# Softmax weights of token tiles 1 to 3 folded into the transposing product by diagonal matrices

## The chip, the cores and the metric

The kernel runs on one core of one Trainium2 chip. The metric is the time of one execution in device microseconds (us), the median of a few runs. The engines are PE (TensorE, matrix products; PEld is its loading of the stationary operand), DVE (VectorE), ACT (ScalarE), POOL (GpSimd, here the issuer of the gathers) and SP (issues the plain DMAs). Each works through its own queue of instructions in order and waits there for semaphores.

## What is computed

One decoder layer over 512 tokens of width 1024: a projection; sparse attention (8 heads in 2 groups of 4, three branches: compressed, selected and window keys, each with a gate) beside a state-space branch; an output projection; and a PEER mixer, in which each token fetches 128 of 16384 experts. What the change touches is the attention's weighting of the values:

```python
def masked_softmax(s, mask):
    s = jnp.where(mask, s, NEG_INF)
    m = jnp.max(s, axis=-1, keepdims=True)
    e = jnp.where(mask, jnp.exp(s - m), 0.0)
    return e / jnp.maximum(jnp.sum(e, axis=-1, keepdims=True), 1e-30)
...
    p_s = masked_softmax(s_s, m_s)
    o_s = jnp.einsum('bghqnk,bgqnkd->bghqd', p_s, v_sel)
...
    return gb[..., 0:1] * o_c + gb[..., 1:2] * o_s + gb[..., 2:3] * o_w
```

With 8 blocks of 64 keys in 512 tokens, all blocks are selected, so the selected branch and the window branch are both causal attention over all earlier keys.

## The kernel before

The tokens stand in four tiles T of 128. Tiles 0 and 1 get their experts by gathers: for each of the 128 experts per token an indirect DMA fetches 128 rows of 8 KB, DVE forms the dot product with the token (`ISA junk`, the row `CUSTOM_DVE_ANT_0` of the profile), ACT the gelu in five small instructions on one column, and DVE adds the weighted value row (`SCALAR_TENSOR_TENSOR X<-X,act`). One such round is called a step here; `peer` (line 1070) makes them, over a ring of five buffers. Tiles 2 and 3 get theirs in `dense` (line 1215), which runs through all experts in 128 rounds and has the steps that are left of tile 1 woven in.

The steps of tile 0 run beside all that tiles 1 to 3 need before their experts: `rest` (line 1461) makes projections, `attention(1)`, the state-space output `glu_out`, the output projection `mix_out`, then, in `later` (line 1512), `attention(2)`, `attention(3)` and the output projection of both, interleaved with `route` of tile 1 (queries, and top-k on DVE), and last `route` of tiles 2 and 3. A credit count (line 1544) says after which piece of `rest` a step is written; it counts pieces, not time. The order on each engine is then set by a scheduler (line 1647), which moves instructions by its own estimate of their durations. All compute instructions are issued by one helper, so the profile gives them all line 134 and they are told apart by tile and shape.

In `attention(T)` (line 692) there are four blocks: two groups g of heads times two branches br. `scores` (line 721) makes for each of four heads the scores in a PSUM bank (PE), their maximum `nm` (DVE), the exponentials `Pt` with their sums `sm` (ACT); then DVE turns `sm` into gate over sum in three small instructions. Then each head's `Pt`, 128 x N with N = 128 (T + 1), is multiplied by its column of `sm`: on ACT for tile 3 and on DVE otherwise (`PSC`, line 688). `pv` (line 745) follows one block later. For each 128 keys it transposes the four heads on PE into one bank, copies the bank to SBUF (`PT`), and multiplies with the values into the bank `O`. `M.S()` gives out a 2 KB slot of a pool that every stage shares; `identb`, `ident` are identity matrices.

Of the kernel before, what the change touches and what calls it, by code (L numbers as in the profile page):

```python
# [18 lines left out]
AF = mybir.ActivationFunctionType  # L19
ALU = mybir.AluOpType  # L20
# [143 lines left out]
def hymba_kernel(ctx: ExitStack, tc: tile.TileContext, a, out, dbg=None):  # L164
    nc = tc.nc
    pins = set()
    V, S, G, PE = (Ordered(tc, e, n, pins) for e, n in ((nc.vector, "V"), (nc.scalar, "S"), (nc.gpsimd, "G"), (nc.tensor, "PE")))
# [10 lines left out]
    def tap(name, src):  # L178
        if name in dbg:
            SP.dma_start(dbg[name], src)  # L180
# [10 lines left out]
    M = Memory([base[:, 8192 * i:8192 * i + 8192] for i in (1, 2, 3, 0)]  # L191
               + [ep.tile([128, 8192], F32, name="X4"), ep.tile([128, 4096], F32, name="X5")])
# [4 lines left out]
    def bank():  # L197
        return pool[0].popleft()

    def bfree(*bs):  # L200
        pool[0].extend(bs)
# [11 lines left out]
    def b3(b, n):  # L213
        return b.rearrange("p (a b) -> p a b", b=n)

    def const(name, shape, dt=F32, eng=None):
        t = cst.tile(shape, dt, name="c_" + name)
        (eng or SP).dma_start(t, a[name])
        return t
# [60 lines left out]
    ident = const("ident", [128, 128])  # L280
# [404 lines left out]
    kcF, vcF = ct("kcF", [128, 2, 31]), ct("vcF", [31, 2, 64])  # L685


    PSC = lambda T, h: T > 2
    PCP = lambda T, kb: T < 3 and kb % 2
    AT, ST, XN, EI, GA = {}, {}, {}, {}, {}  # L690

    def attention(T):
        N = 128 * (T + 1)
        n31 = 7 if T == 0 else 31
        kcT, vcn = (kc0, vc0) if T == 0 else (kcF, vcF)
        ob = bank()
        O = b3(ob, 128)

        pcs = [bank(), bank()]
        for h in range(8):  # L700
            rows = slice(64 * (h % 2), 64 * (h % 2) + 64)
            PE.matmul(b3(pcs[h % 2], 128)[:, h // 2, 0:n31], qT[T][rows, h // 2], kcT[rows, h // 4], start=True, stop=True)
        scl = M.S()
        sc = scl.v([128, 8, n31])
        mx = tiny.tile([128, 8], F32, name="mx")
        sh = [128, 8, n31]
        for par in range(2):
            V.tensor_tensor(sc[:, par::2], b3(pcs[par], 128)[:, :, 0:n31], cmpb[:, T, 0:1, 0:n31].to_broadcast([128, 4, n31]), op=ALU.add)
        bfree(*pcs)
        V.reduce_max(mx, sc, axis=AX.X)  # L710
        V.tensor_tensor(sc, sc, mx[:, :, None].to_broadcast(sh), op=ALU.subtract)
        S.activation(sc, sc, AF.Exp)
        V.tensor_tensor(sc, sc, cmpb[:, T, 1:2, 0:n31].to_broadcast(sh), op=ALU.mult)
        V.reduce_sum(mx, sc, axis=AX.X)
        V.tensor_scalar(mx, mx, 1e-30, None, op0=ALU.max)
        V.reciprocal(mx, mx)
        V.tensor_tensor(mx, mx, gts[:, T, :, 0], op=ALU.mult)
        V.tensor_tensor(sc, sc, mx[:, :, None].to_broadcast(sh), op=ALU.mult)
        yield

        def scores(g, br):
            pl = M.S() if T == 0 else M.L((0, 1))
            Pt = pl.v([128, 4, N])
            nm = tiny.tile([128, 4], F32, name="nm")
            sm = tiny.tile([128, 4], F32, name="sm")
            for h in range(4):
                par, i = h % 2, h // 2
                ps = bank()
                rows = slice(64 * par, 64 * par + 64)
                PE.matmul(ps[:, 0:N], qT[T][rows, 2 * g + i], KT[rows, 2 * br + g, 0:N], start=True, stop=False)  # L730
                PE.matmul(ps[:, N - 128:N], identb, maskb, start=False, stop=True)
                V.reduce_max(nm[:, h:h + 1], ps[:, 0:N], axis=AX.X, negate=True)
                S.activation(Pt[:, h], ps[:, 0:N], AF.Exp, bias=nm[:, h:h + 1], accum_out=sm[:, h:h + 1])
                bfree(ps)
            V.tensor_scalar(sm, sm, 1e-30, None, op0=ALU.max)
            V.reciprocal(sm, sm)
            V.tensor_tensor(sm, sm, gts[:, T, 4 * g:4 * g + 4, 1 + br], op=ALU.mult)
            for h in range(4):
                if PSC(T, h):
                    S.activation(Pt[:, h], Pt[:, h], AF.Copy, scale=sm[:, h:h + 1])  # L740
                else:
                    V.tensor_scalar(Pt[:, h], Pt[:, h], sm[:, h:h + 1], None, op0=ALU.mult)
            return pl, Pt

        def pv(g, br, pl, Pt):
            for kb in range(T + 1):
                b = bank()
                pt = b3(b, 128)
                for h in range(4):
                    PE.transpose(pt[:, 2 * (h % 2) + h // 2], Pt[:, h, kb * 128:kb * 128 + 128], ident)  # L750
                ps = M.S()
                PT = ps.v([128, 4, 128])
                if PCP(T, kb):
                    V.tensor_copy(PT, pt)
                else:
                    S.activation(PT, pt, AF.Copy)
                bfree(b)
                for par in range(2):
                    PE.matmul(O[64 * par:64 * par + 64, 2 * g:2 * g + 2], VC[:, kb, 128 * br + 64 * g:128 * br + 64 * g + 64],
                              PT[:, 2 * par:2 * par + 2], start=(br == 0 and kb == 0), stop=False, skip_group_check=True)  # L760
                M.free(ps)
                yield
            M.free(pl)

        prev = None
        for g in range(2):
            for br in range(2):
                cur = (g, br) + scores(g, br)
                yield
                if prev:  # L770
                    yield from pv(*prev)
                    if prev[1] == 1:
                        yield from cmp_pv(prev[0], sc, vcn, O, n31)
                prev = cur
        yield from pv(*prev)
        yield from cmp_pv(1, sc, vcn, O, n31)
        M.free(scl)
        al = M.S()
        aT = al.v([128, 4, 128])
        S.activation(aT, O, AF.Copy)  # L780
        bfree(ob)
        AT[T] = (al, aT)
        tap(f"aT{T}", aT)
        yield

    def cmp_pv(g, sc, vcn, O, n31):
        b = bank()
        pt = b3(b, 128)
        for h in range(4):
            PE.transpose(pt[0:n31, 2 * (h % 2) + h // 2], sc[:, 4 * g + h], ident)  # L790
        ps = M.S()
        PC = ps.v([n31, 4, 128])
        S.activation(PC, pt[0:n31], AF.Copy)
        bfree(b)
        for par in range(2):
            PE.matmul(O[64 * par:64 * par + 64, 2 * g:2 * g + 2], vcn[:, g], PC[:, 2 * par:2 * par + 2],
                      start=False, stop=True, skip_group_check=True)
        M.free(ps)
        yield
# [851 lines left out]
```

## Time and profile before

| what | value |
| --- | --- |
| median of 3 runs | 1618.69 us (1617.03 to 1622.68) |
| the profiled execution, its own time | 1620.03 us |
| its span, first to last instruction | 1618.2 us |
| DVE busy, share of the span | 91% |
| PE busy, share of the span | 84% |
| ACT busy, share of the span | 52% |
| mean DMA rate | 290 GB/s |

The span falls into a prologue with tile 0 (to about 300 us), the stretch of steps beside `rest` (to about 870 us) and `dense` (the rest). A busy share over the whole span says little about a change that acts between 370 and 600 us; there the stretches have to be read one by one. "PEclk" is the TensorE clock that was granted, as a share of 2.4 GHz: 0.5 is its low level of 1.2 GHz. Records of a PE product end where a model puts it, so back-to-back counts are more to be trusted than single lengths.

### The profile page before, as it was taken

To read this page: it belongs to the slowest core of one execution; us is meant where nothing else is said; L and a number is where in the kernel's file an instruction comes from. 1 tells how busy PE (TensorE), PEld (TensorE's weight loads), DVE (VectorE), ACT (ScalarE), POOL (GpSimd) and SP (SyncE) were. 2 spreads that over 40 slices of the span, in tenths; PEclk is the share of its full clock that TensorE was granted. 3 is DMA by queue.
4 is the path that set the end of the run, shared out by engine and by line. 5 is a ranking of instruction groups with operands and counts; after the bars stand their busy time and mean duration, and the time that the engine had idled before them with its cause. 6 is when DMAs were issued, how large, how long until landed. Compare 5 with 4: busy or idle time off the path is not lost.

```text
span 1618.2 us, 24071 instructions
## 1 busy us (share of the span) xinstructions
PE 1367.1 (84%) x8256; PEld 1081.8 (67%) x8256; DVE 1475.7 (91%) x3392; ACT 837.0 (52%) x2046; POOL 521.8 (32%) x383
## 2 busy tenths in 40 slices
PE   5687794588946689696579999999999999999996
PEld 2366572454433455682358888888888999999995
DVE  8986279969899999699999999999999999999998
ACT  2335523545455675225565555555555556555553
POOL 6422013745354233003002333333333433333331
PEclk9897898787877789899859999999999999999998
DMA  6331478888998989309707999999999999999994
GB/s 263 104 105 65 169 278 295 330 321 300 375 352 297 345 356 370 152 6 343 248 4 262 338 345 332 342 337 340 333 346 357 392 375 377 374 375 379 375 376 171
DMA packets 88967, 469.45 MB, mean 290 GB/s; under 512 B 10253, under 2 KB 10893, under 8 KB 50701
## 3 DMA queue, kind: packets, MB, share of 16 engines
q0 software_dynamic: 37152, 268.98, 42.7%
q1 hardware_dynamic: 51692, 198.94, 34.3%
q8 instruction: 64, 1.05, 0.2%
q14 instruction: 59, 0.48, 0.1%
HBM read 464.74 MB, written 3.15 MB: 289 GB/s over the span
## 4 chain that ended last, share of the span: by engine, by line
DVE 46%; PE 29%; issue 12%; DMA 6%; ACT 3%; POOL 3%; SPq 0%; DVEq 0%; POOLq 0%; ACTq 0%
PE bank L134 29%; DVE X L134 27%; DVE lo L134 8%; DVE junk L134 7%; DMA X<-in_uv,eidx 5%; POOL X L134 2%; ACT X L134 2%; DVE act L134 1%; DVE nm L134 1%; DVE more L134 1%; DMA X<-in_x 0%; ACT gt L134 0%; DMA raw<-in_uvt 0%; DVE zT L134 0%; DVE hid L134 0%
## 5 line engine op out<-in xcount | busy, mean ns | idle before, releaser
L134 POOL DMA_INDIRECT X<-in_uv,eidx x256 | 431.6, 1686 | 967.0 <-DVE X L134 854.1
L134 ACT ACTIVATE X<-bank 128x256 f32<-128x256 f32 (+5 forms) x423 | 213.4, 518 | 184.0 <-PE bank L134 134.3
L134 PE MATMUL bank<-hi,act 128*128 128x512 f32 x1024 | 299.7, 394 | 0.0
L134 PE MATMUL bank<-XH,hi 128*128 128x256 f32 x1024 | 288.9, 282 | 4.1 <-ACT hi L134 4.1
L134 PE MATMUL bank<-XH,lo 128*128 128x256 f32 x1024 | 287.8, 281 | 0.0
L134 PE MATMUL bank<-XL,hi 128*128 128x256 f32 x1024 | 287.5, 281 | 0.0
L134 PE MATMUL bank<-X 128*128 128x64 f16 (+10 forms) x1768 | 235.9, 283 | 59.6 <-DVE X L134 39.7
L134 DVE CUSTOM_DVE_ANT_0 junk<-X 128x1024 bf16<-128x1024 f32 x206 | 250.8, 1217 | 14.0 <-DMA X<-in_uv,eidx 11.0
L134 ACT ACTIVATE gt<-hid 128x1 f32<-128x1 f32 x384 | 63.8, 198 | 363.1 <-DVE hid L134 362.9
L134 DVE TENSOR_TENSOR X<-X 128x256 f32<-128x256 f32 (+13 forms) x611 | 230.6, 410 | 22.5 <-ACT X L134 19.7
L134 DVE SCALAR_TENSOR_TENSOR X<-X,act 128x1024 f32<-128x1024 f32 x194 | 247.6, 1276 | 3.6 <-ACT act L134 3.6
L134 DVE TENSOR_TENSOR lo<-raw,hi 128x1024 fp32r<-128x1024 f32 x172 | 209.4, 1217 | 2.8 <-ACT hi L134 2.8
L134 PEld LDWEIGHTS bank<-hi,act 128*128 128x128 f32 x1024 | 183.3, 188 | 32.6
L134 PEld LDWEIGHTS bank<-XH,hi 128*128 128x128 f32 x1024 | 193.9, 189 | 9.1 <-ACT hi L134 4.2
L134 PEld LDWEIGHTS bank<-XL,hi 128*128 128x128 f32 x1024 | 193.3, 189 | 4.9
L134 PE MATMUL bank<-X,X 128*128 128x128 f32 (+7 forms) x888 | 177.1, 373 | 20.9 <-ACT X L134 12.9
L134 PEld LDWEIGHTS bank<-XH,lo 128*128 128x128 f32 x1024 | 194.2, 190 | 0.0
L134 ACT ACTIVATE hi<-raw 128x1024 fp32r<-128x1024 f32 x172 | 179.0, 1053 | 27.4 <-PE bank L134 21.8
L134 PEld LDWEIGHTS bank<-X,X 128*128 128x128 f32 (+4 forms) x888 | 119.8, 194 | 66.2 <-issue 29.7
L134 PE MATMUL bank<-lo,act 128*128 128x512 f32 x512 | 159.5, 393 | 0.4 <-DVE lo L134 0.4
L134 PEld LDWEIGHTS bank<-X 128*128 128x128 f32 (+3 forms) x744 | 117.5, 197 | 54.9 <-issue 28.5
L134 PE MATMUL bank<-c_ident,X 128*128 128x128 f32 (+2 forms) x300 | 55.6, 337 | 85.4 <-DVE X L134 49.4
(202 smaller groups left out, 1775.2 us busy)
## 6 DMA issues: line engine op xcount, KB each, us to landing
raw<-in_uvt SPq DMA_DIRECT2D x172, 512.0 KB, 7.0
X<-in_uvt SPq DMA_DIRECT2D x84, 512.0 KB, 6.7
X<-in_wq SPq DMA_DIRECT2D x24, 1024.0 KB, 8.9
X<-in_wo SPq DMA_DIRECT2D x8, 1024.0 KB, 7.7
X<-in_x SPq DMA_DIRECT2D x8, 512.0 KB, 3.7
X<-in_wB SPq DMA_DIRECT2D x4, 1024.0 KB, 12.8
X<-in_wA SPq DMA_DIRECT2D x4, 1024.0 KB, 5.2
X<-in_w SPq DMA_DIRECT2D x4, 1024.0 KB, 5.5
```

The lines of the kernel that those rows point to most:

```text
L134: ins = self.last = f(*args, **kw)
```

## The change

For tiles 1 to 3 the weights are no longer multiplied into `Pt`. ACT writes for each head a 128 x 128 matrix with that head's `sm` on its diagonal into a slot `dl` (four heads fill one slot). The transposition on PE becomes an ordinary matrix product of `Pt` with that diagonal matrix, which transposes and weighs at once. Tile 0 stays as it was, on DVE.

```diff
-    PSC = lambda T, h: T > 2
...
+            dl = None if T == 0 else M.S()
             for h in range(4):
-                if PSC(T, h):
-                    S.activation(Pt[:, h], Pt[:, h], AF.Copy, scale=sm[:, h:h + 1])
+                if T == 0:
+                    V.tensor_scalar(Pt[:, h], Pt[:, h], sm[:, h:h + 1], None, op0=ALU.mult)
                 else:
-                    V.tensor_scalar(Pt[:, h], Pt[:, h], sm[:, h:h + 1], None, op0=ALU.mult)
-            return pl, Pt
-
-        def pv(g, br, pl, Pt):
+                    S.activation(dl.v([128, 4, 128])[:, h], ident, AF.Copy, scale=sm[:, h:h + 1])
+            return pl, Pt, dl
+
+        def pv(g, br, pl, Pt, dl):
+
             for kb in range(T + 1):
...
-                    PE.transpose(pt[:, 2 * (h % 2) + h // 2], Pt[:, h, kb * 128:kb * 128 + 128], ident)
+                    o, p = pt[:, 2 * (h % 2) + h // 2], Pt[:, h, kb * 128:kb * 128 + 128]
+                    if T == 0:
+                        PE.transpose(o, p, ident)
+                    else:
+                        PE.matmul(o, p, dl.v([128, 4, 128])[:, h], start=True, stop=True)
...
-            M.free(pl)
+            M.free(pl, *([dl] if dl else []))
```

In the built program DVE has 32 instructions fewer, ACT has 48 diagonals more and 16 multiplications fewer, PE has as many instructions as before, of which 144 have changed from a transposition to a product. The scheduler also puts other work into another order. On PE, at the end of `attention(1)` (`c_ident,X` is a transposition, a 64x256 row is a product with the values, 31x128 rows belong to the compressed branch, X_77 and `more` are slots):

```order
-L134 MATMUL bank_86<-c_ident,X_77 31x128 x3
-L134 MATMUL bank_83<-more,X 64x256 x2
-L134 MATMUL bank_83<-X_77,X 64x256 x2
+L134 MATMUL bank_84<-c_ident,X_77 31x128 x4
+L134 MATMUL bank_86<-c_ident,X_77 31x128 x4
+L134 MATMUL bank_83<-X_77,X 64x256 x4
+L134 MATMUL bank_88<-more,X 128x128 x4
+L134 MATMUL bank_85<-more,X 128x128 x4
 L134 MATMUL bank_83<-X_77,vcF 64x256 x2
-L134 MATMUL bank_86<-c_ident,X_77 31x128
-L134 MATMUL bank_88<-c_ident,X 128x128 x4
-L134 MATMUL bank_85<-c_ident,X 128x128 x4
```

The transposing products of a block (`more` is here the diagonal) now stand ahead of the product with `vcF`, where the transpositions stood behind it; what stands around them is the same stretch of PE work.

On DVE, where `route` of tile 1 ends and the first `MAX` of `route` of tiles 2 and 3 stands; before:

```order
L134 ISA junk,hid<-X 128x1024
L134 ISA hid 128x1
L134 SCALAR_TENSOR_TENSOR ga_2647<-tope,topsum 128x32
L134 TENSOR_TENSOR X_78<-io_136,X_78 128x1024
L134 TENSOR_TENSOR XL<-bank_85,XH 128x4x128
L134 TENSOR_TENSOR X_78<-X_78,X_77 128x1024
L134 TENSOR_TENSOR X_78<-X_78 128x4x128
L134 TENSOR_TENSOR X_78<-X_78 128x4x64
L134 TENSOR_TENSOR X_78<-X_78 128x4x32
L134 TENSOR_TENSOR X_77<-X_78 128x32 x2
L134 SCALAR_TENSOR_TENSOR eidx_2646<-X_77 128x32
L134 MAX X_77<-bank_87 128x8
```

and now (XL, the last of the tiles' transposed copies, stands 11 rows above this piece):

```order
L134 TENSOR_TENSOR X_78<-io_136,X_78 128x1024
L134 TENSOR_TENSOR X_78<-X_78 128x1024
L134 TENSOR_TENSOR X_78<-X_78 128x4x128
L134 TENSOR_TENSOR X_78<-X_78 128x4x64
L134 TENSOR_TENSOR X_78<-X_78 128x4x32
L134 TENSOR_TENSOR X_77<-X_78 128x32 x2
L134 SCALAR_TENSOR_TENSOR eidx_2646<-X_77 128x32
L134 ISA junk,hid<-X 128x1024
L134 ISA hid 128x1
L134 ISA junk,hid<-X 128x1024
L134 ISA hid 128x1
L134 MAX X_78<-bank_87 128x8
```

Between the last XL and the first MAX there now stand the end of one index tree, a whole second one (from io to eidx) and two dot products, where the end of one tree stood. In both programs 113 dot products stand ahead of that MAX.

## Rows read from the trace of the kernel before

**Rows 1.** The page: span, and busy time of each engine.
```profile
span 1618.2 us, 24071 instructions
PE 1367.1 (84%) x8256; PEld 1081.8 (67%) x8256; DVE 1475.7 (91%) x3392; ACT 837.0 (52%) x2046; POOL 521.8 (32%) x383
```

**Rows 2.** Busy time by stretch (columns as its head line says), 376 to 868 us.
```profile
core 0: us, PE busy (x) PEld busy (x) DVE busy (x) ACT busy (x) POOL busy (x), PEclk, DMA share, GB/s
376.00:434.00 58.00, 56.05 (x208) 29.59 (x209) 51.60 (x104) 26.03 (x103) 31.04 (x17) 0.90 0.96 373
434.00:464.00 30.00, 8.09 (x15) 2.64 (x15) 29.13 (x59) 13.62 (x57) 13.28 (x10) 0.51 0.84 316
464.00:514.00 50.00, 35.79 (x194) 23.18 (x195) 49.08 (x105) 30.16 (x111) 19.44 (x14) 0.84 0.88 329
514.00:592.00 78.00, 54.63 (x254) 33.98 (x252) 73.44 (x164) 51.46 (x175) 24.43 (x21) 0.76 0.87 329
592.00:684.00 92.00, 78.86 (x386) 55.67 (x387) 75.90 (x275) 42.01 (x140) 19.65 (x16) 0.93 0.74 297
684.00:868.00 184.00, 142.09 (x973) 103.07 (x972) 176.71 (x727) 92.81 (x217) 22.28 (x20) 0.83 0.41 149
```

**Rows 3.** Waits of DVE, 376 to 684 us: total us, times, longest.
```profile
DVE X L134 <- PE bank L134: 15.2, 1, 15.2
DVE junk L134 <- DMA X<-in_uv,eidx: 7.9, 3, 4.0
DVE X L134 <- ACT act L134: 2.0, 4, 0.8
```

**Rows 4.** Groups by shape, whole span: count | busy us, mean ns | idle before.
```profile
L134 DVE TENSOR_SCALAR X<-X,sm 128x384 f32<-128x384 f32 x16 | 5.7, 415 | 0.0
L134 ACT ACTIVATE X<-X,sm 128x512 f32<-128x512 f32 x16 | 10.2, 710 | 2.3 <-DVE sm L134 2.2
L134 ACT ACTIVATE dg<-c_ident,act 128x128 f32<-128x128 f32 x20 | 8.0, 399 | 1.6 <-PE bank L134 1.1
```

**Rows 5.** The same, DVE from 376 to 514 us, the smaller shape.
```profile
L134 DVE TENSOR_SCALAR X<-X,sm 128x256 f32<-128x256 f32 x16 | 4.5, 335 | 0.0
```

**Rows 6.** The same, PE from 300 to 700 us.
```profile
L134 PE MATMUL bank<-c_ident,X 128*128 128x128 f32 x200 | 38.3, 356 | 66.3 <-DVE X L134 49.1 <-ACT X L134 12.0 <-POOL X L134 5.2
L134 PE MATMUL bank<-X,X 128*128 128x128 f32 x256 | 38.1, 308 | 4.2 <-DMA X<-in_wq 4.2
```

**Rows 7.** Timeline of PE: start, us, what, count, idle before; 376 to 482 us.
```profile
376.33 1.97 PE L134 MATMUL bank<-c_ident,X 128*128 128x128 f32 x8 [1.91 <-DVE X L134]
...
385.61 2.21 PE L134 MATMUL bank<-c_ident,X 128*128 128x128 f32 x12
...
397.49 0.70 PE L134 MATMUL bank<-c_ident,X 128*128 128x128 f32 x4 [1.49 <-DVE X L134]
...
424.81 7.03 PE L134 MATMUL bank<-X,X 128*128 128x512 f32 x16
431.77 1.08 PE L134 MATMUL bank<-kcF,X 64*128 64x31 f32 x16
...
471.40 5.58 PE L134 MATMUL bank<-X,X 128*128 128x128 f32 x48
```

**Rows 8.** Timeline of DVE, about 433 us.
```profile
433.10 0.88 DVE L134 TENSOR_TENSOR X<-bank,X 128x512 f32<-128x512 f32 x2
```

**Rows 9.** Timeline of PE, 560 to 600 us.
```profile
560.03 3.67 PE L134 MATMUL bank<-c_ident,X 128*128 128x128 f32 x16 [6.34 <-ACT X L134]
564.65 3.56 PE L134 MATMUL bank<-c_ident,X 128*128 128x128 f32 x16 [0.94 <-ACT X L134]
...
586.74 3.68 PE L134 MATMUL bank<-c_ident,X 128*128 128x128 f32 x16 [4.73 <-ACT X L134]
592.18 5.50 PE L134 MATMUL bank<-X,X 128*64 128x256 f32 x30 [1.76 <-ACT X L134]
597.51 1.04 PE L134 MATMUL bank<-c_ident,X 128*128 128x128 f32 x8
```

**Rows 10.** The chain that ended last: start, us, what; 580 to 700 us.
```profile
592.18 32.41 PE bank L134 x164
...
662.17 21.27 PE bank L134 x100
```

**Rows 11.** Timeline of DVE, 664 to 686 us.
```profile
664.75 0.68 DVE L134 TENSOR_TENSOR X<-io,X 128x1024 bf16<-128x1024 bf16 x1
...
665.95 0.68 DVE L134 TENSOR_TENSOR X<-X,X 128x1024 bf16<-128x1024 bf16 x1
666.66 1.34 DVE L134 TENSOR_TENSOR X<-X 128x512 bf16<-128x512 bf16 x5
668.04 0.19 DVE L134 SCALAR_TENSOR_TENSOR eidx<-X 128x32 int32<-128x32 f32 x1
683.46 0.30 DVE L134 MAX8 X<-bank 128x8 f32<-128x128 f32 x1 [15.23 <-PE bank L134]
```

## The prediction

> **What bounds the kernel now.** I read the page first [rows 1]: DVE is busy 91% of the span, PE 84%, ACT 52%. The change acts in attention of tiles 1 to 3 alone, so I then cut the time from 376 to 868 us into stretches [rows 2]. The reader is to see three things there. First, DVE is nearly full in every stretch (29.13 of 30, 49.08 of 50, 73.44 of 78 us). The exceptions are the stretch of tile 1, 376 to 434 us (51.60 of 58), and 592 to 684 us (75.90 of 92). Second, PE is full where DVE is not: 56.05 of 58 us at tile 1. From 434 to 464 us it works for 8.09 us only. Third, DMA is not far from its own limit: share 0.96 at tile 1, 0.84 to 0.88 behind it.
>
> The waits of DVE come next [rows 3]. Its one large wait is 15.2 us for PE; gathers cost it 7.9 us in three waits. That 15.2 us ends at 683.46 us with the first MAX8 of route for tiles 2 and 3 [rows 11], and the chain ahead of it lies on PE: 32.41 us from 592.18 and 21.27 us from 662.17 [rows 10]. Behind 684 us DVE is full again (176.71 of 184), with work that the change leaves alone, and so is the last stretch up to the end. So the question is how much sooner that MAX8 can start; from there a shift reaches the end unchanged.
>
> **The change part by part.** DVE loses its 32 multiplications. By the groups' busy time, in which overlaps count once, that is 5.7 us for tile 2 [rows 4] and 4.5 us for tile 1 [rows 5], 10.2 us in all. By the single lengths (16 x 415 and 16 x 335 ns) it would be 12.0 us, but these overlap.
>
> ACT loses tile 3's 16 multiplications, 10.2 us, and gets 48 diagonals. The nearest row is the same instruction of the step, `dg<-c_ident,act`, at 399 ns [rows 4]: at most 48 x 0.40 = 19.2 us, so +9.0 us in all, of which tiles 1 and 2 get 32 x 0.40 = 12.8 us and tile 3 saves 3.8 us. ACT is busy 26.03 of 58 and 30.16 of 50 us where it gets more [rows 2]; I take nothing for it. The cover is the two steps by which an add lies behind its dot product. If the cover is gone, the five gelu instructions of a step queue behind a diagonal that waits for `sm`, and DVE's adds wait for them: that wait is 2.0 us in four times now [rows 3], and eight new blocks at 0.8 us, its longest, would cost 6.4 us.
>
> PE keeps its instruction count, but a transposition is not a product. Of the 204 transpositions of this shape that stand between 300 and 700 us (144 in attention, 36 in the projections, 24 of the normed tokens) the trace has 200 records; of the 128 products of route for tile 1 it has 256 [rows 6]. So an f32 product writes two records where a transposition writes one. Back to back and at the high clock a product's record takes 5.58/48 = 0.116 us [rows 7] and a transposition's at the low clock 3.67/16 = 0.229 us; at the high one 8 of them take 1.04 us [rows 9], 0.13 with the tail of the last. I therefore add one record for each of the 144: 16.7 us at 0.116, 33.0 us at 0.229.
>
> The Trainium skill has two rules that speak against this change. "Perfetto Trace Analysis", section Transposes, wants a logical transpose done as a transpose and not as a standard matmul. "TensorE: Matmul & The Clock Gate", section Terms, gives the transpose mode of trn2 as 4x faster for FP32. By that figure three records' worth would be added for each transposition, an estimate of 3 x 16.7 = 50 us of PE time and not 16.7; the record counts of the rows here bear out a factor of 2 and not 4, and the sum goes by 2.
>
> Now where each of these lies.
>
> *Tile 1 (376 to 434 us).* PE is the end here: after 398 us it has no idle row, its last product of the output projection ends at 431.84, and the DVE addition that needs it starts at 433.10 [rows 7, 8], only 1.3 us later. Of 32 transpositions (28 on record) the first eight run at the low clock (1.97/8 = 0.246 us), the others at up to 0.18. So PE gets 8 x 0.229 + 24 x 0.116 = 4.6 us more. Against that stand the 1.3 us of slack and about half of the 1.5 us that PE waits at 397.49 for DVE's scaling: 4.6 - 1.3 - 0.75 = +2.5 us. DVE's 4.5 us are not gained here, because DVE will wait for PE (and gathers run at a share of 0.96). Bounds: -4.5 (DVE was the end after all) and +6.8 (32 x 0.229 less half a microsecond). I take +2.5, the row that PE's own timeline gives.
>
> *Tile 2 (464 to 514 us).* DVE is full, PE has 14 us free and waits for DVE, so 5.7 us go and the 48 x 0.116 = 5.6 us of PE hide in PE's idle time. But steps run on here and gathers at share 0.88: I let a fifth of the gain go back into waits for gathers, -4.6. Bounds: -5.7, and +5.6 if PE's part is exposed and DVE's part lost.
>
> *Tile 3 (514 to 600 us).* DVE saves nothing here. PE's 64 transpositions stand in four blocks, three of them at the low clock [rows 9], behind waits for ACT's multiplication of 6.34, 0.94 and 4.73 us and one of 1.76 for a copy, together 13.8 us; those three blocks' extra 48 x 0.229 = 11.0 us can hide in the waits, since a diagonal (0.40) replaces a 710 ns multiplication [rows 4] ahead of them. The fourth block lies in the full PE stretch from 592 us: 16 x 0.116 = +1.9 us. Bounds: -3.8 (ACT's saving in the chain) and +12.9 (nothing hidden).
>
> *The end (660 to 684 us).* In the new order one more index tree and two dot products stand between the last XL and the first MAX on DVE. By the rows of a tree (0.68 + 0.68 + 1.34 + 0.19 = 2.9 us, its end 1.5) and two dots of about 1.25 that is 1.5 + 2.9 + 2.5 = 6.9 us where 2.2 us stood (0.68 + 1.34 + 0.19) [rows 11]. The difference of 4.7 us would fill part of the 15.2 us in which DVE waits there. PE has to get to route as much sooner for that, with 28 products of route for tile 1 now between the transpositions of the two normed tiles; I take -4.0. Bounds: -4.7 and 0.
>
> *The slots.* `dl` holds up to two more 2 KB slots at a time, and the order shows two of the 24 loads of route's queries moved to another buffer. PE's wait for such a load is 4.2 us now [rows 6]; I take 0, bounds -1 and +4.2.
>
> Sum: 2.5 - 4.6 + 1.9 - 4.0 = -4.2 us. The profiled execution took 1620.03 us (span 1618.2, and 1.8 around it), 1.3 us above the median of the runs; 1620.0 - 4.2 = 1615.8 for such an execution, 1618.7 - 4.2 = 1614.5 for the median.
>
> **The rivals.**
>
> *DVE alone decides.* The whole 10.2 us go and the end gives its 4.7: -14.9, 1603.8 us. For it: from 434 to 668 us DVE hardly waits, and the chain names PE at 592 us although DVE was busy all along. Against: PE's timeline at tile 1, and gathers at 0.96.
>
> *PE becomes the bound at tile 3.* Its products run at the low clock, as three blocks do now, and the waits ahead of them shrink by half only, as ACT still has to be waited for: 12.9 - 6.9 = +6.0, with +2.5 at tile 1 and -2.6 left at tile 2, and nothing at the end, since route starts later: +5.9, 1624.6 us. It decides from the point where the added PE time exceeds the 13.8 us of waits it can replace. For it: granted clock 0.76 from 514 to 592 us, PE solid from 592 us, the chain on PE there. Against: the granted clock is 0.93 from 592 us, where PE is solid [rows 2], and ACT's part is shorter.
>
> *Nothing comes through.* The gathers pace the steps: 113 dot products stand ahead of that MAX in both orders, and DMA is at 0.84 to 0.96. DVE's gain turns into waits for gathers: 1618.7, give or take 3. Against: only 7.9 us of such waits now.
>
> **How the numbers follow.** Forecast 43%, DVE alone 20%, PE bound 25%, nothing 12%. About 0.3% (4.9 us) is what a measurement of this kernel can tell from no change. The forecast's own spread is -10 to +1, so half of its 43 is faster by more than that and half within; DVE alone is faster; of the PE bound 23 are slower and 2 within; nothing is within. Faster 0.42, same 0.35, slower 0.23. The range takes in most of every case: 1602 (DVE alone, 2 us further) to 1627 (PE bound, 2.4 us further); some 15% lie outside. The forecast alone is 1608 to 1620.
>
> **What would show it.** Right: DVE has no `X<-X,sm` of 256 or 384 columns; ACT has 48 of `X<-c_ident,sm` at up to 0.40 us; PE has 288 records for the 144 products at 0.116 or 0.229 each; DVE waits some microseconds for PE about 435 us; the wait at the first MAX8 of route 2 and 3 has shrunk to about 11 us. Wrong: the wait at that MAX8 is gone or has grown, the tile 1 stretch ends sooner than before, or from 514 to 600 us DVE waits for PE. The stretch behind 684 us must keep its length; if it doesn't, the order there, which I take as neutral, has cost or gained something.

## The result and the profile after

The changed kernel took 1611.95 us (median of 10 runs, 1604.20 to 1616.77), the kernel before 1621.97 us beside it (10 runs, 1617.03 to 1627.73). The ratio is 0.9931 with a 95% interval of 0.9909 to 0.9952, so -11.2 us (-14.8 to -7.8); it is not the quotient of the two medians, which is 0.9938. Two later measurements gave 0.9931 and 0.9927. The range of the prediction holds the time and its likeliest direction was right, but its centre does not fit: -4.2 us would be a ratio of 0.9974, outside the interval. "DVE alone decides" (-14.9 us, 0.9908) lies just outside the interval's other edge. The truth is between the two, nearer to that rival. That the time is only 2.5 us from the forecast's 1614.5 is in part luck: the kernel before took 3.3 us more beside it than in the runs that the forecast started from (1621.97 for 1618.69). The range is 25 us wide and took in all rivals, so that it holds the time says little about the mechanism.

The page of the kernel after, whose span is that of one execution (1615.0 us, the slowest of its ten):

```profile
span 1615.0 us, 24342 instructions
PE 1387.1 (86%) x8400; PEld 1101.2 (68%) x8400; DVE 1466.9 (91%) x3360; ACT 839.7 (52%) x2078; POOL 526.7 (33%) x383
```

Against [rows 1] PE has 144 records and 20.0 us more, DVE 32 instructions and 8.8 us less, ACT 32 instructions and 2.7 us more. The 20.0 us belong to this execution. In a second one of the same kernel PE has 10.0 us more than in [rows 1], in a third (1376.0 us) 8.9; the records are as many:

```profile
PE 1377.1 (86%) x8400; PEld 1094.5 (68%) x8400; DVE 1465.6 (91%) x3360; ACT 839.2 (52%) x2078; POOL 526.8 (33%) x383
```

The groups by shape, ACT over the whole span and then PE from 300 to 700 us (count | busy us, mean ns | idle before):

```profile
L134 ACT ACTIVATE X<-c_ident,sm 128x128 f32<-128x128 f32 x44 | 13.9, 388 | 1.2 <-DVE X L134 0.6 <-DVE sm L134 0.5
```

```profile
L134 PE MATMUL bank<-X,X 128*128 128x128 f32 x528 | 78.0, 312 | 4.2 <-DMA X<-in_wq 4.2
L134 PE MATMUL bank<-c_ident,X 128*128 128x128 f32 x56 | 10.1, 329 | 36.9 <-DVE X L134 34.6 <-POOL X L134 2.3
L134 PE MATMUL bank<-more,X 128*128 128x128 f32 x16 | 2.1, 281 | 0.0
```

The diagonals are there (44 in this row, the other four are written into a slot named `more`), at 388 ns. Where [rows 6] had 256 product records there are 528 + 16 = 544, so 288 for 144 products, two each; the transpositions fell from 200 to 56 records.

One execution of each kernel is a poor comparison here: the two spans, 1618.2 and 1615.0 us, differ by 3.2 us only, because this execution of the changed kernel was a long one. So what follows uses several executions of each: of the kernel before a second one (before_again), of the changed kernel two more (after_again, after_c).

To see where the time went I cut each trace at marks in its own program: first maximum of the scores of tile 1; 25 us later; first and last maximum of tile 2; last maximum of tile 3; first MAX8 of `route` of tiles 2 and 3; first `lo` of `dense`; end. The stretches of the kernel before (start:end and length, busy time of each engine, PEclk, DMA share, GB/s):

```profile
core 0: us, PE busy (x) PEld busy (x) DVE busy (x) ACT busy (x) POOL busy (x), PEclk, DMA share, GB/s
350.96:375.96 25.00, 21.10 (x93) 12.93 (x93) 19.14 (x46) 14.90 (x49) 7.12 (x5) 0.64 0.51 182
375.96:435.29 59.33, 57.34 (x211) 30.27 (x212) 52.93 (x107) 27.14 (x106) 31.44 (x17) 0.90 0.96 371
435.29:499.02 63.73, 36.11 (x178) 20.94 (x177) 61.94 (x123) 35.78 (x139) 25.33 (x19) 0.74 0.89 334
499.02:583.52 84.50, 57.44 (x264) 34.91 (x264) 82.07 (x186) 52.35 (x184) 30.38 (x24) 0.76 0.84 312
583.52:683.46 99.94, 82.00 (x398) 58.43 (x399) 81.75 (x288) 48.01 (x156) 20.70 (x17) 0.90 0.77 309
683.46:797.20 113.74, 85.25 (x338) 55.00 (x336) 110.02 (x584) 46.69 (x163) 18.24 (x18) 0.95 0.50 184
797.20:1618.19 820.99, 780.93 (x5600) 702.14 (x5600) 796.81 (x1188) 471.49 (x837) 254.42 (x125) 0.96 0.87 326
```

The same stretches of the changed kernel, second execution (after_again):

```profile
350.36:375.36 25.00, 22.78 (x99) 14.79 (x100) 18.73 (x45) 16.70 (x58) 7.13 (x5) 0.64 0.51 173
375.36:431.58 56.22, 56.22 (x239) 31.89 (x239) 47.76 (x90) 28.79 (x111) 28.39 (x16) 0.98 0.98 386
431.58:491.81 60.23, 40.10 (x223) 26.30 (x224) 57.55 (x118) 37.01 (x145) 23.83 (x18) 0.74 0.88 336
491.81:568.72 76.91, 58.48 (x310) 36.35 (x309) 76.91 (x178) 50.36 (x181) 28.85 (x23) 0.82 0.87 319
568.72:675.80 107.08, 85.50 (x425) 61.07 (x424) 88.84 (x289) 47.86 (x174) 26.97 (x20) 0.89 0.80 322
675.80:786.36 110.56, 86.14 (x338) 55.34 (x336) 108.03 (x582) 44.91 (x162) 19.24 (x18) 0.93 0.50 191
786.36:1608.38 822.02, 780.29 (x5600) 701.15 (x5600) 797.63 (x1191) 472.48 (x838) 255.97 (x125) 0.96 0.87 325
```

Length minus DVE's busy time is what DVE idles in a stretch (59.33 - 52.93 = 6.40, and so on). That splits every gain or loss into DVE's work and DVE's waiting. The same subtraction for all five executions:

| DVE idle, us | before | before_again | after | after_again | after_c | forecast of the difference |
| --- | --- | --- | --- | --- | --- | --- |
| first 25 us of tile 1 | 5.9 | 5.9 | 5.8 | 6.3 | 5.9 | 0 |
| rest of tile 1 | 6.4 | 7.1 | 13.6 | 8.5 | 8.6 | +7.0 (4.5 + 2.5) |
| tile 2 | 1.8 | 1.0 | 5.4 | 2.7 | 4.3 | +1.1 (5.7 - 4.6) |
| to the last maximum of tile 3 | 2.4 | 2.7 | 0.0 | 0.0 | 0.0 | +1.9 |
| to the first MAX8 | 18.2 | 20.9 | 15.6 | 18.2 | 16.7 | -4.0 |
| to `dense` | 3.7 | 4.6 | 3.0 | 2.5 | 2.5 | 0 |
| DVE idle, sum | 38.4 | 42.1 | 43.5 | 38.2 | 38.0 | +6.0 |
| DVE busy, sum | 407.8 | 407.7 | 398.5 | 397.8 | 397.9 | -10.2 |
| tile 1 to `dense` | 446.2 | 449.8 | 442.0 | 436.0 | 435.9 | -4.2 |

DVE's work fell by 10 us, as the sum had it. Its waiting did not grow by 6 us: in two of the three executions it is no longer than before, in the first it is 1 to 5 us longer. `dense` itself takes 1.0 us more (821.0 before, 822.0 to 822.2 after). With idle at 38.1 in those two against a mean of 40.2, that is -10 - 2 + 1 = -11 us, about the measured difference; with the first execution in the mean it is some 2 us less.

Where the executions of the changed kernel differ most is one row, the rest of tile 1. This is the first execution, and then after_c:

```profile
375.87:437.11 61.24, 61.24 (x237) 34.38 (x236) 47.61 (x90) 28.42 (x109) 25.47 (x16) 0.88 0.92 347
```

```profile
374.46:430.18 55.72, 55.53 (x237) 30.98 (x236) 47.08 (x89) 28.30 (x109) 28.34 (x16) 0.99 0.99 384
```

PE is busy without a gap in the first and but for 0.2 us in the other; at a granted clock of 0.88 the stretch takes 61.24 us, at 0.99 55.72 us. The first is as the prediction had it (+1.9 us on before's 59.33, where it said +2.5). The other, like after_again, is the usual case in the traces here: 3.1 to 4.2 us shorter than before's two (59.33, and 59.95 in before_again).

At the end of `route` of tile 1 the wait ahead of the first MAX8, 15.23 us in [rows 11], is shorter in the first execution after (DVE's timeline: start, us, idle before in brackets), and DVE's waits for PE from 376 to 684 us are 19.5 us where [rows 3] had 15.2 (total, times, longest):

```profile
681.85 0.30 DVE L134 MAX8 X<-bank 128x8 f32<-128x128 f32 x1 [11.23 <-PE bank L134]
```

```profile
DVE X L134 <- PE bank L134: 19.5, 11, 11.2
```

The other ten waits, 8.3 us together, are new; 6.4 us of them lie at tile 1, between 376 and 437 us. Over the whole window the maxima (`nm`) waited for PE for another 6.1 us, where it was 1.5 before. The usual executions look otherwise: from 376 to 684 us these two rows have 15.6 and 1.6 us in after_again, 14.4 and 2.5 in after_c, together hardly more than before.

At tile 1 itself DVE never waited for PE in the kernel before (376 to 434 us); in after_again (375 to 432 us) it does, beside new waits for ACT:

```profile
DVE junk L134 <- DMA X<-in_uv,eidx: 4.0, 1, 4.0
DVE X L134 <- ACT act L134: 2.0, 4, 0.8
```

```profile
DVE X L134 <- ACT X L134: 2.5, 3, 1.2
DVE X L134 <- PE bank L134: 2.1, 3, 1.6
DVE junk L134 <- DMA X<-in_uv,eidx: 1.9, 2, 1.3
DVE X L134 <- ACT act L134: 1.2, 1, 1.2
```

### The profile page after: what moved, and what is told of

It is laid out like the page before. It is cut to its first block, busy times and chain, and to the rows that moved or that the text cites. A ratio compares the mean times of both kernels' runs of the same rounds, so it can differ in the third digit from the quotient of the medians.

```text
span 1615.0 us, 24342 instructions
## 1 busy us (share of the span) xinstructions
PE 1387.1 (86%) x8400; PEld 1101.2 (68%) x8400; DVE 1466.9 (91%) x3360; ACT 839.7 (52%) x2078; POOL 526.7 (33%) x383
## 4 chain that ended last, share of the span: by engine, by line
DVE 25%; PE 22%; issue 4%; ACT 1%; DMA 0%; SPq 0%
PE bank L134 22%; DVE X L134 11%; DVE lo L134 8%; DVE junk L134 3%; DVE act L134 1%; DMA raw<-in_uvt 0%; ACT X L134 0%; DVE f_r L134 0%; DVE hid L134 0%; ACT hi L134 0%; ACT junk L134 0%; SPq L1240 0%; ACT raw L134 0%; DVE more L134 0%; ACT act L134 0%
## 5 line engine op out<-in xcount | busy, mean ns | idle before, releaser
L134 POOL DMA_INDIRECT X<-in_uv,eidx x256 | 434.8, 1698 | 955.4 <-DVE X L134 814.0
L134 ACT ACTIVATE X<-bank 128x256 f32<-128x256 f32 (+5 forms) x431 | 218.4, 520 | 194.0 <-PE bank L134 141.8
L134 PE MATMUL bank<-X 128*128 128x64 f16 (+10 forms) x1800 | 248.1, 288 | 71.9 <-DVE X L134 51.4
L134 DVE TENSOR_TENSOR X<-X 128x256 f32<-128x256 f32 (+14 forms) x627 | 234.8, 409 | 22.7 <-ACT X L134 19.9
L134 PE MATMUL bank<-X,X 128*128 128x128 f32 (+5 forms) x1172 | 216.4, 360 | 21.7 <-ACT X L134 11.8
L134 PEld LDWEIGHTS bank<-X,X 128*128 128x128 f32 (+3 forms) x1172 | 154.8, 201 | 69.4 <-issue 30.3
L134 PEld LDWEIGHTS bank<-X 128*128 128x128 f32 (+3 forms) x776 | 125.9, 200 | 69.4 <-issue 31.3
L134 PEld LDWEIGHTS bank<-lo,act 128*128 128x128 f32 x512 | 96.0, 188 | 22.7 <-DVE lo L134 0.8
```

Source lines behind the costliest of these rows:

```text
L134: ins = self.last = f(*args, **kw)
```

## The experiments

All ratios are to the kernel before, run on the same chip between the runs of the experiment, with 95% intervals; 0.001 is 1.6 us. Two theories stood at the start: the sum by stretches, as predicted, and that DVE alone decides.

**The two kernels once more.** No edit.

> The changed kernel itself, for a second profile and a ratio beside the runs below. Both theories: ratio to before 0.991 to 0.995. The theory by stretches (PE bounds tile 1, DVE tile 2, PE's full stretch a part of tile 3, and the end gives some 4 us back) expects the second profile like the first: DVE waits for PE at tile 1, about 11 us ahead of the first MAX8 of route 2 and 3. The rival (DVE alone decides: 10.2 us of DVE work less) expects no more waits of DVE than before, in this profile too.

Measured: 1610.48 us, 0.9931 (0.9907 to 0.9955).

> The kernel before, for a second profile: how much the stretches of one and the same program differ from profile to profile. Both theories: ratio 1.000 within 0.003, and the waits of DVE at the same places as in the first profile.

Measured: 1619.65 us, 0.9986 (0.9968 to 1.0004), which is how far a kernel may stand from itself here.

**One tile at a time, and two.** The diagonals only where T is in a list; otherwise the code of before.

```diff
-            dl = None if T == 0 else M.S()
+            dl = M.S() if T in (1,) else None          # (2,)   (3,)   (1, 2)
...
-                if T == 0:
-                    V.tensor_scalar(Pt[:, h], Pt[:, h], sm[:, h:h + 1], None, op0=ALU.mult)
+                if T not in (1,):
+                    if T > 2:
+                        S.activation(Pt[:, h], Pt[:, h], AF.Copy, scale=sm[:, h:h + 1])
+                    else:
+                        V.tensor_scalar(Pt[:, h], Pt[:, h], sm[:, h:h + 1], None, op0=ALU.mult)
```

Tile 1 alone (d1):

> Diagonals for tile 1 alone. By stretches: PE bounds tile 1, so its products cost and DVE's 4.5 us are not gained: +2.5 us against before (0 to +4). DVE alone: -4.5 us. The run with tiles 1 and 2 gained 14 us, more than either had it; if the rest is a matter of the new order, d1 and d2 need not add up to it.

Measured: 1616.13 us, 0.9951 (0.9936 to 0.9965), -8.0 us, more than either theory had for it. Its row for the rest of tile 1:

```profile
377.61:433.79 56.18, 56.18 (x237) 31.55 (x236) 47.37 (x90) 28.22 (x109) 28.62 (x16) 0.97 0.98 383
```

56.18 us, 3.1 to 3.8 less than before and like the usual execution of the changed kernel, again with PE solid and a clock of 0.97. The sum had a loss of 2.5 us for this tile. This is the step that falls. Where the rest of the 8.0 us lies the trace does not show: this execution was the slowest of its twelve (1621.26 us), it takes 446.3 us from tile 1 to `dense` where the kernel before takes 446.2 and 449.8, and the wait ahead of the first MAX8 is as long as before:

```profile
685.67 0.30 DVE L134 MAX8 more<-bank 128x8 f32<-128x128 f32 x1 [15.12 <-PE bank L134]
```

Tile 2 alone (d2):

> Diagonals for tile 2 alone. By stretches: -4.6 us, with up to -4 more at the end: -5 to -9. DVE alone: -5.7 us, and -10 with the end.

Measured: 1610.50 us, 0.9919 (0.9892 to 0.9946), -13.1 us, more than the 5.7 us of DVE work it takes away. In its trace the wait ahead of the first MAX8 is 7.69 us, half of before's.

```profile
674.31 0.30 DVE L134 MAX8 X<-bank 128x8 f32<-128x128 f32 x1 [7.69 <-PE bank L134]
```

So tile 2 by itself shortens this wait more than all three tiles do (10.2 to 11.6 us there). But -5.7 for the work and -7.5 for the wait (15.2 to 7.7) may not simply be added up: in the stretch of tile 2 DVE now idles 7.1 us, where it idled 1.8 and 1.0 before. From tile 1 to `dense` it idles 36.0 us (38.4 and 42.1 before) and works 3.2 us less, and the span, 1610.3 us, is 8 us shorter than before's two. What makes up the whole of -13.1 us is not shown.

Tile 3 alone (d3):

> Diagonals for tile 3 alone; DVE has as many instructions as before. By stretches: +1.9 at tile 3, up to -4 at the end: -2 to +2 us against before. DVE alone: 0. A third reading of the changed kernel's trace (the XL copies 12 us earlier, because ACT's 10.2 us of multiplications are gone from the chain of tile 3) expects -4 to -8 us.

Measured: 1624.22 us, 1.0012 (0.9989 to 1.0035), +1.9 us by the middle, no difference that can be told. The prediction had +1.9 for this tile; the third reading, -4 to -8, is outside the interval (-1.8 to +5.7). From the last maximum of tile 2 to the first MAX8 it takes 192.2 us, where the kernel before takes 184.4 and 187.4; but a part of that is work that stood behind the MAX8, and up to `dense` it is 302.6 us against 298.2 and 302.1:

```profile
497.24:598.49 101.25, 69.42 (x315) 44.38 (x316) 97.68 (x209) 59.78 (x222) 37.96 (x30) 0.70 0.88 325
598.49:689.48 90.99, 82.69 (x414) 59.77 (x413) 68.02 (x266) 35.89 (x119) 16.04 (x11) 0.94 0.74 268
```

Tiles 1 and 2 (d12, d12_again):

> Diagonals for tiles 1 and 2; tile 3 keeps ACT's multiplication and the transposition. By stretches: +2.5 at tile 1, -4.6 at tile 2, up to -4 at the end: -2 to -6 us against before. DVE alone: all of DVE's 10.2 us are gained here, -10 us or more, as fast as the whole change.

Measured: 1605.55 us, 0.9914 (0.9884 to 0.9944), -14.0 us.

> The version with diagonals for tiles 1 and 2 once more, beside the changed kernel on the same chip. If tile 3's diagonals cost something, as that tile alone suggested (+2 us), it is 2 to 4 us faster than the changed kernel; if the two differ by order alone, within 1 us of it.

Measured: 1606.26 us, 0.9927 (0.9894 to 0.9959), -11.8 us, with the changed kernel at 0.9927 beside it:

> The changed kernel once more, for the comparison with the version that has diagonals for tiles 1 and 2: about 0.993 to the kernel before, as in the two measurements before.

Measured: 1609.46 us, 0.9927 (0.9900 to 0.9955). The medians of the version without tile 3 are 4.9 and 3.2 us below the changed kernel's in the two measurements, but the ratios do not part: whether tile 3's diagonals cost anything in company with the others stays open. No run shows that they gain anything.

The parts do not add up. -8.0, -13.1 and +1.9 would be -19.2; together they give -11.2. Tiles 1 and 2 give -14.0 and -11.8 where the parts give -21.1. Why is not shown. It is not that tiles 1 and 2 share the wait ahead of the MAX8: d2 and d12 halve it (7.7, then 7.6 and 7.2 us), but d1 leaves it at 15.1. A part can be chance, as the intervals are wide (d1 5.7 to 10.4 us, d2 8.8 to 17.5, d12 9.1 to 18.8 and 6.7 to 17.2).

**PE's cost alone (pe_only).** The weights as before, on DVE and ACT; the 144 transpositions as products with the identity.

```diff
-                        PE.matmul(o, p, dl.v([128, 4, 128])[:, h], start=True, stop=True)
+                        PE.matmul(o, p, ident, start=True, stop=True)
```

> PE's part alone: the weights are multiplied in as before (DVE for tiles 1 and 2, ACT for tile 3), and the 144 transpositions become products with the identity matrix, two records each. By stretches: about +3 at tile 1, 0 at tile 2, +1.9 to +6 at tile 3: +5 to +9 us against before. DVE alone: 0. If all of PE's time counted: +16.7 us.

Measured: 1632.15 us, 1.0067 (1.0043 to 1.0092), +10.9 us. Tile 1's rest and the stretch to the last maximum of tile 3:

```profile
374.29:439.14 64.85, 60.16 (x241) 34.70 (x241) 53.35 (x107) 27.23 (x106) 34.66 (x17) 0.93 0.96 360
502.67:598.72 96.05, 70.44 (x335) 43.87 (x336) 89.09 (x193) 57.89 (x205) 35.48 (x27) 0.75 0.85 313
```

At tile 1 DVE idles 64.85 - 53.35 = 11.5 us, 4.4 to 5.1 more than before, about the 4.6 us that the prediction had put on PE there. That is the cost beside the old scaling, and PE has gaps in this stretch, 64.85 - 60.16 = 4.7 us, where the changed kernel's PE has 0 to 0.2. By the trace its first wait is for DVE's scaling (it begins ahead of the stretch), the longest for ACT:

```profile
375.20 3.78 PE L134 MATMUL bank<-c_ident,X 128*128 128x128 f32 x16 [1.90 <-DVE X L134]
...
410.25 5.66 PE L134 MATMUL bank<-X,X 128*64 128x256 f32 x16 [3.20 <-ACT X L134]
```

How many of the gaps are the scaling's fault is not shown.

**DVE's share alone (nw12).** The kernel before without the 32 multiplications of tiles 1 and 2; their weights are missing in its result.

```diff
                 if PSC(T, h):
                     S.activation(Pt[:, h], Pt[:, h], AF.Copy, scale=sm[:, h:h + 1])
-                else:
+                elif T == 0:
                     V.tensor_scalar(Pt[:, h], Pt[:, h], sm[:, h:h + 1], None, op0=ALU.mult)
```

> The kernel before without the 32 multiplications of tiles 1 and 2 on DVE (their weights are left out of the result); transpositions and tile 3 as before, no diagonals. If DVE's time is what decides, it gains as much as the version with diagonals for tiles 1 and 2 did (-14 us, 0.991) or more, since PE and ACT have less to do. If PE's products cost what the sum put them at (4.6 + 5.6 us, a part of it hidden), it gains some 3 to 5 us more than that version: 0.988 to 0.989. If it gains clearly less (0.995), the larger part of -14 us is a matter of order.

Measured: 1608.15 us, 0.9927 (0.9900 to 0.9955), -11.8 us: what the changed kernel gains, to the last digit of the ratio, and what d12 gains within its interval. So the work taken from DVE is enough for the whole gain, and the products and diagonals, which the changed kernel has on top, cost nothing that can be told within the 4.5 us to either side that these intervals leave. The 3 to 5 us that this run was to gain over d12, had PE's products cost what the sum put them at, did not show. At tile 1:

```profile
375.39:426.43 51.04, 50.68 (x194) 26.98 (x192) 43.26 (x81) 25.29 (x98) 18.49 (x14) 0.97 0.98 361
```

With transpositions and no scaling the stretch takes 51.04 us, 5 us less than with products (56.2 in d1 and after_again). PE has 45 records fewer in it than in after_again, of which 32 are the products', so they account for the larger part and not for all. This lead of 5.2 us over after_again (56.22 - 51.04) has shrunk to 1.2 us where `dense` begins (434.8 us from the first maximum of tile 1, against 436.0): only 111 dot products stand ahead of the first MAX8 in this order, 113 in the changed kernel, and the stretch behind it takes 117.70 us instead of 110.56.

**All weights left out (no_weights).** Tiles 1 to 3 get neither multiplication nor diagonal; their weights are missing in the result.

```diff
                 if T == 0:
                     V.tensor_scalar(Pt[:, h], Pt[:, h], sm[:, h:h + 1], None, op0=ALU.mult)
-                else:
-                    S.activation(dl.v([128, 4, 128])[:, h], ident, AF.Copy, scale=sm[:, h:h + 1])
...
-                    if T == 0:
-                        PE.transpose(o, p, ident)
-                    else:
-                        PE.matmul(o, p, dl.v([128, 4, 128])[:, h], start=True, stop=True)
+                    PE.transpose(pt[:, 2 * (h % 2) + h // 2], Pt[:, h, kb * 128:kb * 128 + 128], ident)
```

> Left out: for tiles 1 to 3 the weights are not multiplied in anywhere (no diagonals, no multiplication on DVE or ACT), and PE transposes as before. That is the change with its DVE part and without its PE and diagonal part. DVE alone: about as fast as diagonals for tiles 1 and 2, -10 to -15 us. By stretches: -4.6 to -5.7 at tile 2, 0 to -1.5 at tile 1, -4 at the end, and some microseconds of ACT at tile 3: -10 to -14 us. If PE's extra time costs the changed kernel anything, this run is faster than the changed kernel by as much.

Measured: 1611.48 us, 0.9936 (0.9912 to 0.9960), -10.4 us. Without any of this work the kernel is no faster than with diagonals and products, within the intervals.

**Slots and order alone (slots_only).** The kernel before, with `dl` taken and freed and never written.

```diff
+            dl = None if T == 0 else M.S()
+            return pl, Pt, dl
...
-            M.free(pl)
+            M.free(pl, *([dl] if dl else []))
```

> The kernel before with the same instructions; a slot dl is taken for every block of tiles 1 to 3 and freed with its block, and nothing is written to it. So only the slots, and through them the order that the scheduler writes, differ. If the order by itself is worth several us either way, the ratio leaves 1 by 0.3% or more (the differences of several us between the parts and the whole would then be differences of order). If what the parts gain is the work taken away, it is within 0.2% of 1.

Measured: 1620.04 us, 0.9993 (0.9973 to 1.0014). The order did change, and stretches with it: the stretch of tile 3 takes 10 us longer than in the kernel before, the two behind it 7 and 3 us less (110.71 for 113.74 in the second), and the sum stays.

```profile
503.07:597.56 94.49, 64.91 (x288) 34.39 (x288) 91.30 (x207) 59.05 (x209) 37.99 (x28) 0.71 0.84 306
597.56:690.40 92.84, 77.87 (x376) 55.95 (x377) 72.61 (x264) 40.00 (x132) 16.37 (x14) 0.89 0.77 302
```

This one other order is worth nothing by itself. It also warns against reading one stretch of two differently ordered programs as a gain: DVE does 91.30 us of work in the first of these rows and 82.07 in before's. What the stretch got longer by is work that stood elsewhere.

## Why the prediction was right and wrong

*What DVE, ACT and PE gain and lose* held. DVE's busy time from tile 1 to `dense` fell by 9.2 to 10.0 us (forecast 10.2). A product has two records. PE's busy time on the page grew by 20.0 us in the first execution and by 19.9 in pe_only (1387.0 us), within the 16.7 at the high clock and 33.0 at the low one; in the usual executions of the changed kernel it grew by 10.0 and 8.9 only, where more of PE's work ran at the high clock (mean clock 0.916 and 0.914, against 0.908 in the first execution). ACT's diagonals took 13.9 us for 44, 388 ns each by length, below the 0.40 us that was allowed, and ACT grew by 2.7 us on the page against at most 9.0. What ACT makes DVE wait for was put at nothing and is not: from 376 to 684 us DVE's adds wait 4.2 to 5.2 us for `act`, where they waited 2.0, and 2.5 to 2.7 us for other work of ACT, for which they did not wait before. The diagonals need not be the reason, since nw12 has none and waits 5.0 and 1.8 us. On the rules weighed: the Trainium skill ("TensorE: Matmul & The Clock Gate", section Terms) has the transpose mode 4x faster for FP32, by which PE would have grown by an estimated 50 us; the traces show 8.9 to 20.0 us and two records for one, a factor of 2 in records. And "Perfetto Trace Analysis", section Transposes, is borne out by pe_only, where products instead of transpositions cost 10.9 us with nothing in return; it does not decide here, where the product also carries the weights.

*Tile 1, +2.5 us,* is the step that failed. Alone the tile gained 8.0 us (5.7 to 10.4), and the rest of tile 1, 59.3 and 60.0 us before, became 55.7 to 56.2 in the usual execution. That PE is the end there holds for the changed kernel, where it has no gap to speak of; in the kernel before the prediction inferred it from 1.3 us of slack, while DVE's waits there were 4.0 us for gathers and 2.0 for ACT and none for PE. In the usual execution DVE waits 2.1 to 2.4 us for PE at tile 1, and its idling grew by 1.7 to 1.9 us over the mean of before's two instead of 7.0, so most of DVE's 5 us were gained after all. The size of PE's new work was about right (forecast 4.6, pe_only 4.4 to 5.1 us more of DVE idling). What was wrong, by the traces, is to treat PE's stretch as full at a given clock, and to give the scaling that goes away only half of one wait (0.75 us). Take busy time times granted clock as PE's work at full clock: before 57.34 x 0.90 = 51.6 us out of 59.33, so 7.7 us went to gaps and low clock; after_again 56.22 x 0.98 = 55.1 out of 56.22, so 1.1 us. The work grew by 3.5 us and the losses fell by 6.6 us (rough by about 1 us: the same product of the first execution after is 53.9, of after_again 55.1). In the execution where the clock stayed low longer (61.24 x 0.88 = 53.9, losses 7.3 us) the losses stayed and the forecast came true, with DVE idling 13.6 us where 6.4 + 7.0 = 13.4 were forecast. The row that should have warned is in [rows 7]: the first transposition waits 1.91 us for the scaling with the clock at its low level, and I counted only the later wait of 1.49.

That the clock rose early because the wait is gone is the likely reading, not a shown one. The five executions with the old scaling and transpositions at tile 1 (before, before_again, slots_only, d2, d3) have 0.90 or 0.91 in this stretch; of the six with diagonals five have 0.97 to 0.99 and one 0.88; nw12, without scaling and with transpositions, has 0.97. But no_weights, which has no scaling either, has 0.87, and pe_only, which has it, 0.93, so that the products themselves play a part is not ruled out.

*Tile 2, -4.6 us,* was too much in its own stretch. DVE's work there fell by 4.0 to 4.4 us (61.9 to 57.6 and 57.9), its idling grew by 1.3 to 4.0 us over the mean of before's two (1.4), where 1.1 was forecast, so the stretch became 0 to 3 us shorter. Alone the tile gave far more, -13.1; a shorter wait at the end is a part of it.

*Tile 3, +1.9 us*: alone it was +1.9 by the middle of its interval (-1.8 to +5.7). In company no wait of DVE shows there; DVE is busy in 76.91 of 76.91 us. The bound of +12.9 and the rival "PE becomes the bound at tile 3" (1624.6) did not come, and pe_only shows its mechanism in part only: with products beside the old multiplications DVE idles 96.05 - 89.09 = 7.0 us there, against 2.4 and 2.7, of which the trace puts one wait of 2.6 us down to PE and 4.3 us to gathers.

*The end, -4.0 us*, held roughly: the wait ahead of the first MAX8 is 11.2, 11.6 and 10.2 us for 15.2 and 15.7, where "about 11" was forecast, and the idle time up to it fell by 1 to 4 us. It could have been less: d12 has 7.6 and 7.2, d2 7.7, nw12 5.8.

*The slots, 0*: slots_only gives 0.9993. *Behind the MAX8, 0*: the stretch to `dense` became about 3 us shorter, 2 of them work that now stands ahead of the MAX8 (110.0 to 108.0 us of DVE), and `dense` 1 us longer.

*The rivals.* "Nothing comes through" was wrong: DVE's waits for gathers from 376 to 684 us fell, 2.8 us in after_again and 3.0 in after_c where [rows 3] has 7.9. "DVE alone decides" is the better account: nw12 gains as much from DVE's work alone. Why PE's longer work then costs nothing is argued and not shown; at tile 1 the likely cover is gaps and low clock that went away. Of the 4.7 us that it added at the end 2.7 came (the idle time up to the MAX8, 19.5 to 16.8 us in the means). Of the three things that were to speak against the forecast one showed, the one that matters: the tile 1 stretch ends sooner than before, in two of the three executions.

What stays open: why the clock stayed low longer in one execution; why products beside the old weights cost 10.9 us and beside diagonals nothing that can be told; how much of d1's, d2's and d12's time is luck of the order; whether tile 3 is better left alone.

## What to carry over

What it is worth to take work off one engine depends on what the others do beside it: without DVE's multiplications (10.2 us of busy time) the kernel gained 11.8 us beside transpositions (nw12), and 22 us beside products (pe_only's 1.0067 to 0.9931), there together with tile 3's multiplications on ACT. Before a stretch of PE is called full, multiply its busy time by its granted clock and ask what the engine would do at the full one. And where a scheduler rewrites the order, split each stretch into work and idle time of the engine that bounds it, add up to a mark that all programs share, and take several executions: parts tried one by one need not add up.

## What the runs showed of the hardware

The same program, at the same time to 0.01 us, got the high clock in one execution and not yet in the other. PE's timeline of the first execution after, and then of after_again (start, us, what, count):

```profile
374.13 3.73 PE L134 MATMUL bank<-X,X 128*128 128x128 f32 x16
377.79 1.22 PE L134 MATMUL bank<-X 64*128 64x256 f32 x2
...
382.95 1.22 PE L134 MATMUL bank<-X 64*128 64x256 f32 x2
```

```profile
374.12 3.63 PE L134 MATMUL bank<-X,X 128*128 128x128 f32 x16
377.68 0.70 PE L134 MATMUL bank<-X 64*128 64x256 f32 x2
```

Both had the same row of scores and products ahead without a gap; from 377.7 us the pair of score products takes 1.22 us in the one and 0.70 in the other. From 376 to 388 us PE is busy without a gap in both, at a granted clock of 0.50 in the first and 0.94 in after_again (length, PE busy, PEclk, DMA share, GB/s):

```profile
376.00:388.00 12.00, 12.00 (x41) 0.50 0.90 339
```

```profile
376.00:388.00 12.00, 12.00 (x58) 0.94 0.91 345
```

The rest of tile 1 takes 5.0 us longer in the first (61.24 against 56.22), most of the 6.6 us between the two spans. Over whole runs of one and the same kernel time goes with the granted clock too: in 18 runs of the kernel before, beside the last experiments, the correlation of time and mean clock is -0.89, 0.9 us for each 0.001 of clock. That the clock is the cause of all of that spread is not shown.
